# Block 2's feed-forwards in parts of 4, 6, 6 and 6 chunks, and the down weights' lower parts by an accumulating DMA

## Chip, cores and metric

One core of one Trainium2 chip. The metric is the device time in microseconds of one execution; the kernel before was run three times. The matmuls run on TensorE (PE); VectorE (DVE), ScalarE (ACT) and GpSimd (POOL) work beside it, SyncE (SP) issues loads. All names of rows are the program's.

## The reference, cut to what matters

Two transformer blocks in fp32 on 512 tokens, model width 1024. Block 1 sets 16 further tokens ahead of them (528 columns), block 2 has 512. Each block is a feed-forward, a mixer and a second feed-forward, so there are four feed-forwards (FFN1 and FFN2 in block 1, FFN3 and FFN4 in block 2), each 2816 wide:

```
D_FF = 2816
def swiglu_2(x, w_gate, w_up, w_down):
    return (jax.nn.silu(x @ w_gate) * (x @ w_up)) @ w_down
...
h = h + 0.5 * swiglu_2(rms_norm(h, ffn1_norm[l]), ffn1_w_gate[l], ffn1_w_up[l], ffn1_w_down[l])
...
h = h + 0.5 * swiglu_2(rms_norm(h, ffn2_norm[l]), ffn2_w_gate[l], ffn2_w_up[l], ffn2_w_down[l])
```

## The kernel before, in words

**Numbers in two parts.** Every fp32 operand is held as an upper part (hi, rounded to fp32r) and a lower part (lo, the rest), and each product is three matmuls: hi by hi, hi by lo, lo by hi (`mm`, L482; rows of L488). For a weight, ACT copies the raw block into hi (L120). The lower part is made in one of two ways. In the feed-forwards DVE subtracts hi from raw (L125). In the mixers, where `lo_engine` is `None`, ACT writes the negated copy of the raw (rounded like hi) into lo (L122), and a DMA that POOL issues adds the raw to it (L123, `accum_op=add`).

**The queue of weights.** `Weights` holds a list of raws in the order of use. Two raw buffers (raw_85, raw_86) take them in turn, and raw r+2 is loaded when the last unit of raw r is split. A unit (one 128-column weight block) is split by `pump` (L107) as soon as a slot, a pair of hi and lo buffers, is idle; a slot becomes idle when the matmuls of its unit are done (`free`, `release`). In the stretches of this change three whole slots turn, in the rows whi_106 with wlo_107, whi_108 with wlo_109, whi_110 with wlo_111 (and the wide pair 112/113 in FFN4); two more are cut into halves for the sevens.

**A feed-forward.** The 2816 rows are 22 chunks of 128. `PARTS` (L24) cuts them into 6, 8 and 8. For each chunk the gate and up sums are formed, `evac` makes silu(gate) times up and splits it into gh and gl; after a part's chunks, `down` (L785) multiplies them by the part's rows of the down weight: 8 column blocks, each 3 matmuls per chunk into `dn`, whose sum is added to h (`add_h`, L1321; in block 1 to y, `sum_y`, L885). `add_down` (L325) lists 4 raws with 2 units each per part.

The chunks of part 0 are full products (`run_item`: 48 matmuls of 512 columns in block 2). The chunks of later parts go by sevens (`seven`, L703): 7 products of 256-column halves in place of 8, 84 matmuls of 256 (`product`, L696; rows of L700). Their right-hand sides are made once by `prepare` (L661): 8 `normed` steps, 2 splits, 2 differences, 4 `second` steps, and 4 more splits into nh and nl, called `rest`. nh and nl hold part 0's right-hand side, so `rest` must come behind part 0's last item. In `seven` the first product's sum is copied by ACT (`ht`, L736) and the product named P6 follows in the same PSUM tile.

At the end of a part by sevens, `begin` (L775) starts the first down units on all chunks but the last while the last chunk is still being finished: one and one more in block 2, one and two more in FFN1 with its two column slices. `down` then finishes them.

**The order.** `run_ffn` (L543) runs the items left over from the lead, with `prepare`'s steps spread over the last of them, then `rest`, `down(0)`, the sevens of part 1, `down(1)` and the sevens of part 2, whose down the caller runs beside the next stage. A tile scheduler then orders each engine's instructions; that order is what the engines keep.

## Time and profile before

| what | value |
| --- | --- |
| median of three runs | 2034.89 us (2034.45 to 2038.19) |
| the profiled execution | 2036.98 us, of which its span is 2035.2 us |
| mean granted TensorE clock | 0.994 of full speed |
| instructions in the profile | 34893 |
| HBM read | 230.53 MB |

In the rows, "hi" and "lo" are tiles whi and wlo, "raw" is a weight as loaded, "dn" and "acc" are PSUM sums. Rows name an engine, a line of the program, an operation and its tile: `out<-in`.

### The profile page before, as it was taken

The page shows a single profiled execution, that of the slowest core. Times are in us where ns is not written, and L with a number is a line of the kernel's source. Part 1 is how long each engine was busy: PE and PEld are TensorE (multiplying, and loading weights), DVE is VectorE, ACT ScalarE, POOL GpSimd, SP SyncE. Part 2 cuts the span into 40 slices and gives each one's busy share as a digit, 9 for nine tenths or more (in the row PEclk, how much of TensorE's full clock was granted, in tenths as well). Part 3 has the DMA queues.
Part 4 walks back from the last instruction along what each step waited for, and adds up shares of the span by engine and source line. Part 5 has one row for each costly group of instructions (what it writes and reads, how often), then busy time and mean ns, then how long its engine had stood idle before and what let it go on. Part 6 is the DMA issues. An engine that isn't in the chain of part 4 may idle for free.

```text
span 2035.2 us, 34893 instructions
## 1 busy us (share of the span) xinstructions
PE 1995.0 (98%) x13583; PEld 1833.5 (90%) x13583; DVE 1486.4 (73%) x2949; ACT 1063.4 (52%) x2030; POOL 283.2 (14%) x290
## 2 busy tenths in 40 slices
PE   8999999999999999999999999999999999999998
PEld 8999999989989989899998998987777788898998
DVE  5948578777776767668777775876889868685784
ACT  5445345357765445445443543656878743353552
POOL 0012021023420002111000211103211100120210
PEclk9999999999999999999999999999999999999999
DMA  6357575237784238566532766737545353475761
GB/s 182 93 116 166 131 149 147 84 81 174 149 147 125 73 93 166 146 139 157 151 78 78 162 149 140 156 116 159 102 98 114 76 152 99 108 162 140 147 163 44
DMA packets 413212, 260.10 MB, mean 128 GB/s; under 512 B 17483, under 2 KB 405830, under 8 KB 413046
## 3 DMA queue, kind: packets, MB, share of 16 engines
q1 hardware_dynamic: 317446, 192.94, 32.1%
q0 software_dynamic: 95040, 63.69, 22.1%
q8 instruction: 106, 1.74, 0.3%
q10 hardware_dynamic: 560, 1.24, 0.2%
q14 instruction: 60, 0.49, 0.1%
HBM read 230.53 MB, written 4.23 MB: 115 GB/s over the span
## 4 chain that ended last, share of the span: by engine, by line
PE 84%; DVE 8%; ACT 4%; DMA 2%; issue 1%; POOL 0%; ACTq 0%; POOLq 0%; DVEq 0%; SPq 0%
PE dn L488 25%; PE sa L700 18%; PE acc L488 14%; PE sc L700 8%; PE sb L700 4%; PE accB L488 3%; PE accA L488 3%; PE wo L488 2%; DVE wlo L125 1%; ACT whi L120 1%; PE ro L1611 1%; PE p L423 1%; PE num L1202 1%; PE ms L1469 1%; DMA raw<-in_w_uq 1%
## 5 line engine op out<-in xcount | busy, mean ns | idle before, releaser
L120 ACT CAST whi<-raw 128x1024 fp32r<-128x1024 f32 (+3 forms) x500 | 397.5, 801 | 346.3 <-PE dn L488 168.5
L125 DVE TENSOR_TENSOR wlo<-raw,whi 128x512 fp32r<-128x512 f32 (+2 forms) x456 | 406.2, 905 | 134.7 <-ACT whi L120 130.6
L488 PE MATMUL dn<-gh,whi 128*128 128x256 f32 (+2 forms) x908 | 277.5, 326 | 0.6 <-ACT gh L469 0.6
L488 PE MATMUL dn<-gl,whi 128*128 128x256 f32 (+2 forms) x908 | 277.9, 326 | 0.0
L488 PE MATMUL dn<-gh,wlo 128*128 128x256 f32 (+2 forms) x908 | 277.0, 325 | 0.0
L488 PE MATMUL acc<-nh,whi 128*128 128x512 f32 (+2 forms) x600 | 191.0, 353 | 1.1 <-DVE y L1219 1.1
L488 PE MATMUL acc<-nl,whi 128*128 128x512 f32 (+2 forms) x600 | 188.5, 349 | 0.0
L488 PE MATMUL acc<-nh,wlo 128*128 128x512 f32 (+2 forms) x600 | 188.1, 348 | 0.0
L488 PEld LDWEIGHTS dn<-gh,whi 128*128 128x128 f32 x908 | 163.0, 188 | 16.5 <-ACT gh L469 0.8
L488 PEld LDWEIGHTS dn<-gl,whi 128*128 128x128 f32 x908 | 163.1, 188 | 15.5 <-DVE gl L470 0.3
L488 PEld LDWEIGHTS dn<-gh,wlo 128*128 128x128 f32 x908 | 163.2, 188 | 14.8
L700 PE MATMUL sc<-nh,whi 128*128 128x256 f32 (+1 forms) x488 | 137.4, 282 | 0.0
L700 PE MATMUL sa<-nh,whi 128*128 128x256 f32 (+1 forms) x488 | 137.3, 281 | 0.0
L700 PE MATMUL sa<-nh,wlo 128*128 128x256 f32 (+1 forms) x488 | 137.2, 281 | 0.0
L700 PE MATMUL sc<-nh,wlo 128*128 128x256 f32 (+1 forms) x488 | 137.2, 281 | 0.0
L700 PE MATMUL sc<-nl,whi 128*128 128x256 f32 (+1 forms) x488 | 137.1, 281 | 0.0
L700 PE MATMUL sa<-nl,whi 128*128 128x256 f32 (+1 forms) x488 | 137.0, 281 | 0.0
L488 PEld LDWEIGHTS acc<-nh,whi 128*128 128x128 f32 (+1 forms) x600 | 104.6, 188 | 16.4 <-DVE y L1219 1.6
L488 PEld LDWEIGHTS acc<-nh,wlo 128*128 128x128 f32 (+1 forms) x600 | 104.0, 188 | 15.0
L488 PEld LDWEIGHTS acc<-nl,whi 128*128 128x128 f32 (+1 forms) x600 | 103.9, 188 | 13.6
L95 POOL DMA_DIRECT2D raw<-in_ffn_w_up x32 | 41.1, 1284 | 448.8 <-DMA raw<-in_ffn_w_up 229.1
L95 POOL DMA_DIRECT2D raw<-in_ffn_w_in x32 | 41.1, 1283 | 439.4 <-DMA raw<-in_ffn_w_in 163.6
(494 smaller groups left out, 5583.1 us busy)
## 6 DMA issues: line engine op xcount, KB each, us to landing
raw<-in_ffn_w_in SPq DMA_DIRECT2D x56, 512.0 KB, 4.1
raw<-in_ffn_w_gate SPq DMA_DIRECT2D x44, 512.0 KB, 3.6
raw<-in_ffn_w_in SPq DMA_DIRECT2D x64, 256.0 KB, 3.2
raw<-in_ffn_w_out SPq DMA_DIRECT2D x16, 1024.0 KB, 8.0
wlo<-raw POOLq DMA_DIRECT2D x32, 512.0 KB, 5.3
raw<-in_ffn_w_up SPq DMA_DIRECT2D x64, 256.0 KB, 3.2
raw<-in_ffn_w_down SPq DMA_DIRECT2D x16, 1024.0 KB, 7.4
raw<-in_a_w_in SPq DMA_DIRECT2D x18, 512.0 KB, 3.6
```

What stands on the lines that cost most here:

```text
L95: self.nc.gpsimd.dma_start(out=dst(t), in_=src, accum_op=ALU.add)
L120: nc.scalar.copy(out=ho, in_=src)
L125: self.lo_engine.tensor_tensor(out=lw, in0=src, in1=ho.bitcast(F32), op=ALU.subtract)
L423: pe.matmul(self.p1[:, self.n:self.n + 2], lhsT=src[:, o:o + P], rhs=ones[:, 0:2], start=True, stop=True)
L488: pe.matmul(p, lhsT=w[:, k], rhs=cut(x, k, sl), start=(k == 0 and j == 0), stop=(k == last and j == 2))
L700: pe.matmul(acc, lhsT=w[:, 4 * i + k], rhs=x[:, k], start=start and k == 0 and j == 0, stop=k == 3 and j == 2, skip_group_check=not start)
L1202: pe.matmul(num[:, c0:SEQ], lhsT=w[0:kk, j], rhs=x[s_], start=(j == 0 and i == 0), stop=(j == 4 and i == 2))
L1469: pe.matmul(s, lhsT=mq[i][a][:, t0:t0 + P], rhs=mk[i][b], start=j == 0, stop=j == 2)
L1611: pe.matmul(o[i], lhsT=vt_[:, i, j], rhs=s_[i, j][b], start=(j == 0 and b == 0), stop=(j == 3 and b == 1))
```

## The change

It has two parts. First, FFN3 and FFN4 take `PARTS4`, 4, 6, 6 and 6 chunks, so that 18 of their 22 chunks go by sevens in place of 16, with four downs in place of three. With four items in part 0, three or two are used up in the lead; `run_ffn` then has one or two left, calls `prepare` before any of them, spreads the 8 `normed` steps over them, and hands the 12 other steps to `down(0)`, which runs two behind each of the first six column blocks. Second, `add_down` gets `by_dma`: in all four feed-forwards the down units of every part but the last have their lower part made as in the mixers.

```
+PARTS4 = [(0, 4), (4, 6), (10, 6), (16, 6)]
...
-    def add(self, loads, subs, halves=(), more=()):
+    def add(self, loads, subs, halves=(), more=(), by_dma=False):
...
-                if self.lo_engine is None:
+                if self.lo_engine is None or self.raws[r][3]:
                     nc.scalar.activation(out=lw, in_=src, func=ACTF.Copy, scale=-1.0)
                     nc.gpsimd.dma_start(out=lw.bitcast(F32), in_=src, accum_op=ALU.add)
                 else:
                     self.lo_engine.tensor_tensor(out=lw, in0=src, in1=ho.bitcast(F32), op=ALU.subtract)
...
-            add_down(d_ap, f0, nf)
+            add_down(d_ap, f0, nf, f0 < parts[-1][0])
...
-        run_item(items[0], slices)
+        if len(items) > 2:
+            run_item(items.pop(0), slices)
...
+        under = len(steps) if ffn.parts is PARTS else KD
...
+            down(0, (), steps[did:] + rest)
...
-        for part in (1, 2):
-            first = ffn.seven(range(PARTS[part][1]), slices if part == 1 else last)
-            if part == 1:
-                down(1, first)
+        n = len(ffn.parts) - 1
+        for part in range(1, n + 1):
+            first = ffn.seven(range(ffn.parts[part][1]), slices if part < n else last)
+            if part < n:
+                down(part, first)
...
                 for p, sl in zip(pp, slices):
                     sink(c, sl, p)
+                for f in steps[:each]:
+                    f()
+                del steps[:each]
                 W.free(1)
```

Whole program, instructions in the engines' lists: PE 13050 to 13146, DVE 2728 to 2706, ACT 1837 to 1974, POOL 281 to 369, SP 404 to 420. Of POOL's 88 more, 80 are the DMAs of L123 (8 units for each part that has them) and 8 those of the four further chunks by sevens.

**First place: ACT and POOL in the down of FFN3's second part.** Before, ACT's list where the down's units are split (the one 128x512 row belongs to the sevens that follow):

```order
L120 CAST whi_108<-raw_86 128x1024
L120 CAST whi_110<-raw_85 128x1024
L120 CAST whi_106<-raw_85 128x1024
L120 CAST whi_108<-raw_86 128x1024
L120 CAST whi_116<-raw_85 128x512
L120 CAST whi_110<-raw_86 128x1024
```

With the change:

```order
L122 CAST whi_108<-raw_86 128x768
L124 ACTIVATE wlo_109<-raw_86 128x768
L122 CAST whi_110<-raw_85 128x768
L124 ACTIVATE wlo_111<-raw_85 128x768
L122 CAST whi_106<-raw_85 128x768
L124 ACTIVATE wlo_107<-raw_85 128x768
L122 CAST whi_108<-raw_86 128x768
L124 ACTIVATE wlo_109<-raw_86 128x768
L122 CAST whi_110<-raw_86 128x768
L124 ACTIVATE wlo_111<-raw_86 128x768
```

Each copy into hi is followed by the negated copy of the same raw, and a unit now has 6 blocks of 128 columns where it had 8. POOL's list with the change, from the last loads of the sevens to the end of this down:

```order
L97 DMA raw_86<-in_ffn_w_up 128x4x128
L97 DMA rawx_12017<-in_ffn_w_gate 128x4x128
L125 DMA wlo_107<-raw_86 128x6x128
L125 DMA wlo_109<-raw_86 128x6x128
L125 DMA wlo_111<-raw_85 128x6x128
L125 DMA wlo_107<-raw_85 128x6x128
L125 DMA wlo_109<-raw_86 128x6x128
L125 DMA wlo_111<-raw_86 128x6x128
```

Before, POOL's list held only the accumulating loads of the sevens at this place:

```order
L95 DMA rawx_11984<-in_ffn_w_gate 128x4x128
L95 DMA rawx_11983<-in_ffn_w_gate 128x4x128
L95 DMA rawx_11984<-in_ffn_w_gate 128x4x128
L95 DMA raw_85<-in_ffn_w_up 128x4x128
L95 DMA raw_86<-in_ffn_w_up 128x4x128
```

So six DMAs of L125 stand in a row where POOL had nothing to issue, and two more just ahead of the piece.

**Second place: PE in the down of FFN1's second part,** from its fourth unit on (slot 110/111; the three units before were begun ahead of the last chunk). Before:

```order
L488 MATMUL dn<-gl,whi_110 128x272
L488 MATMUL dn<-gl,whi_110 128x256
L488 MATMUL dn<-gh,whi_106 128x272
L488 MATMUL dn<-gh,whi_106 128x256
L488 MATMUL dn<-gl,whi_106 128x272
L488 MATMUL dn<-gl,whi_106 128x256
L488 MATMUL dn<-gh,wlo_111 128x272
L488 MATMUL dn<-gh,wlo_111 128x256
```

With the change:

```order
L490 MATMUL dn<-gh,whi_106 128x272
L490 MATMUL dn<-gh,whi_106 128x256
L490 MATMUL dn<-gl,whi_106 128x272
L490 MATMUL dn<-gl,whi_106 128x256
L490 MATMUL dn<-gh,whi_108 128x272
L490 MATMUL dn<-gh,whi_108 128x256
L490 MATMUL dn<-gl,whi_108 128x272
L490 MATMUL dn<-gl,whi_108 128x256
L490 MATMUL dn<-gh,wlo_111 128x272
L490 MATMUL dn<-gh,wlo_111 128x256
```

Before, 8 matmuls (4 of the fourth unit, 4 of the fifth) stand ahead of the first that reads wlo_111; now 12 do (4 of the sixth too).

**Third place: DVE in FFN3's first down.** Before, the lower parts of the down's units and the sums into h:

```order
L1323 TENSOR_TENSOR h<-dn,h 128x512
L125 TENSOR_TENSOR wlo_107<-raw_85,whi_106 128x768
L1323 TENSOR_TENSOR h<-dn,h 128x512
L125 TENSOR_TENSOR wlo_109<-raw_86,whi_108 128x768
L1323 TENSOR_TENSOR h<-dn,h 128x512
```

With the change, the steps of `prepare` (ht, y, wlowide, nl) stand there:

```order
L1336 TENSOR_TENSOR h<-dn,h 128x512
L472 TENSOR_TENSOR wlowide<-ht,whiwide 128x256
L692 SCALAR_TENSOR_TENSOR ht<-y 128x256 x2
L694 SCALAR_TENSOR_TENSOR y<-ht,y 128x256
L472 TENSOR_TENSOR wlowide<-ht,whiwide 128x256
L694 SCALAR_TENSOR_TENSOR y<-ht,y 128x256
L1336 TENSOR_TENSOR h<-dn,h 128x512
L472 TENSOR_TENSOR wlowide<-ht,whiwide 128x256
L472 TENSOR_TENSOR nl<-y,nh 128x4x256 x2
L1336 TENSOR_TENSOR h<-dn,h 128x512
L472 TENSOR_TENSOR nl<-y,nh 128x4x256 x2
L127 TENSOR_TENSOR wlo_109<-raw_85,whi_108 128x1024
```

The last row is the first lower part of the sevens that follow; it stands behind the last of the splits into nl.

## Rows read from the trace of the kernel before

**Rows 1.** The page: busy time of each engine, and the chain that ended last.

```profile
PE 1995.0 (98%) x13583; PEld 1833.5 (90%) x13583; DVE 1486.4 (73%) x2949; ACT 1063.4 (52%) x2030; POOL 283.2 (14%) x290
...
PE 84%; DVE 8%; ACT 4%; DMA 2%; issue 1%; POOL 0%; ACTq 0%; POOLq 0%; DVEq 0%; SPq 0%
```

**Rows 2.** Busy times by stretch: us, PE, PEld, DVE, ACT, POOL, PEclk, DMA share, GB/s.

```profile
1054.00:1088.00 34.00, 34.00 (x151) 27.64 (x150) 32.36 (x68) 16.32 (x30) 2.57 (x2) 1.00 0.36 85
1088.00:1121.00 33.00, 33.00 (x144) 26.74 (x143) 19.97 (x30) 9.61 (x15) 0.54 (x1) 1.00 0.31 94
1121.00:1200.00 79.00, 78.59 (x651) 77.13 (x650) 63.90 (x121) 45.98 (x96) 17.59 (x14) 1.00 0.76 157
1207.50:1247.00 39.50, 39.50 (x173) 32.04 (x172) 18.41 (x25) 9.94 (x13) 3.85 (x3) 1.00 0.51 130
...
1598.60:1604.30 5.70, 4.64 (x24) 3.29 (x22) 5.27 (x11) 5.58 (x13) 2.77 (x3) 1.00 0.74 92
```

**Rows 3.** Timeline of PE, FFN3: first matmul of a stage (start us, us, row).

```profile
1054.23 0.48 PE L488 MATMUL acc<-nh,whi 128*128 128x512 f32 x1
1087.68 0.39 PE L488 MATMUL dn<-gh,whi 128*128 128x512 f32 x1
1121.08 0.28 PE L700 MATMUL sa<-xh,whi 128*128 128x256 f32 x1
1247.16 0.28 PE L700 MATMUL sa<-xh,whi 128*128 128x256 f32 x1
```

**Rows 4.** Timeline, FFN3's second part: its down's fourth unit on ACT, DVE, PE.

```profile
1213.04 2.00 ACT L120 CAST whi<-raw 128x1024 fp32r<-128x1024 f32 x2 [3.03 <-PE dn L488]
1214.58 2.35 DVE L125 TENSOR_TENSOR wlo<-raw,whi 128x1024 fp32r<-128x1024 f32 x2
1219.36 0.39 PE L488 MATMUL dn<-gh,whi 128*128 128x512 f32 x1
```

**Rows 5.** Timeline of ACT and POOL in block 2's mixer; issue to landing there.

```profile
1570.24 1.07 ACT L122 ACTIVATE wlo<-raw 128x1024 fp32r<-128x1024 f32 x1
...
1571.60 1.57 POOL L123 DMA_DIRECT2D wlo<-raw  x1 [7.75 <-ACT wlo L122]
...
DMA to landing us min/median/max: 5.7/5.8/5.9
```

**Rows 6.** DMA issues by tile, KB each, median us to landing, here and there.

```profile
raw<-in_ffn_w_gate SPq DMA_DIRECT2D x44, 512.0 KB, 3.6
...
raw<-in_ffn_w_down SPq DMA_DIRECT2D x16, 1024.0 KB, 7.4
...
wlowide<-raw POOLq DMA_DIRECT2D x1, 512.0 KB, 11.6
```

**Rows 7.** Instructions by line and form, 1054 to 1121 us: busy, mean ns, idle before.

```profile
L125 DVE TENSOR_TENSOR wlo<-raw,whi 128x768 fp32r<-128x768 f32 x8 | 7.6, 950 | 0.4 <-ACT whi L120 0.4
...
L651 DVE TENSOR_TENSOR a<-acc,r_bc 128x256 f32<-128x256 f32 x6 | 2.3, 415 | 0.0
...
L120 ACT CAST whi<-raw 128x768 fp32r<-128x768 f32 x8 | 6.7, 836 | 15.4 <-PE dn L488 10.5 <-PE acc L488 4.9
```

**Rows 8.** Timeline, FFN1's second part: its down's fourth unit and first unit.

```profile
229.10 2.95 ACT L120 CAST whi<-raw 128x1024 fp32r<-128x1024 f32 x3 [8.41 <-PE dn L488]
...
230.59 0.40 PE L488 MATMUL dn<-gh,whi 128*128 128x272 f32 x2
230.83 0.41 PE L488 MATMUL dn<-gl,whi 128*128 128x272 f32 x2
...
203.74 0.37 ACT L736 COPY ht<-sa 128x264 f32<-128x264 f32 x1
210.60 0.41 PE L488 MATMUL dn<-gh,wlo 128*128 128x272 f32 x2
```

**Rows 9.** Timeline, FFN2's second part: ACT's `ht` and the down's first unit.

```profile
831.40 0.37 ACT L736 COPY ht<-sa 128x256 f32<-128x256 f32 x1
...
837.91 0.39 PE L488 MATMUL dn<-gh,wlo 128*128 128x512 f32 x1
```

**Rows 10.** Timeline of PE: the last chunk's P6 product in FFN3, FFN4.

```profile
1194.18 0.39 PE L700 MATMUL sa<-whiwide,whi 128*128 128x256 f32 x1 [0.16 <-ACT ht L736]
1840.91 0.39 PE L700 MATMUL sa<-whi,whi 128*128 128x256 f32 x1 [0.52 <-ACT ht L736]
```

More of the change, by code (lines that the diff above doesn't have):

```diff
@@ L556, in run_ffn @@
             w_half, n_half = [(w4, 1)], 2
[L557 removed]
+        if len(items) > 2:
+            run_item(items.pop(0), slices)
         slots += [W.reserved.pop(0) for _ in range(3 - len(slots))]
         steps, rest = ffn.prepare(halves, gcol, xn, slots)
[L560 to L562 removed]
+        under = len(steps) if ffn.parts is PARTS else KD
+        did = 0
+        for i, it in enumerate(items):
+            upto = under * (i + 1) // len(items)
             run_item(it, slices, steps=steps[did:upto])
@@ L632, in two_blocks, with __init__ @@
     class Ffn:
-        def __init__(self, name, half, wide=256):
+        def __init__(self, name, half, wide=256, parts=PARTS):
+            self.parts = parts
             self.cm, self.p = open_pool(name)
@@ L639, in items @@
         def items(self, part):
-            return [Item(2, lambda sl, a, f=f: self.evac(f, sl, a[0], a[1])) for f in range(PARTS[part][1])]
+            return [Item(2, lambda sl, a, f=f: self.evac(f, sl, a[0], a[1])) for f in range(self.parts[part][1])]
         def evac(self, f, sl, g, u):
@@ L783, in finish, with down @@
             mm(list(zip(pp, slices)), u, [nf - 1], (self.gh, self.gl), last=nf - 1)
-        def down(self, nf, slices, sink, first=()):
-            first = list(first)
+        def down(self, nf, slices, sink, first=(), steps=()):
+            first, steps = list(first), list(steps)
+            each = -(-len(steps) // KD)
             for c in range(KD):
@@ L976, in two_blocks @@
         dve.tensor_scalar(out=g, in0=g, scalar1=0.5, scalar2=None, op0=ALU.mult)
-    first = run_ffn(ffn, items[3:], AB, lambda part, first: ffn.down(PARTS[part][1], AB, sum_y(part == 0), first),
+    first = run_ffn(ffn, items[3:], AB, lambda part, first, steps=(): ffn.down(ffn.parts[part][1], AB, sum_y(part == 0), first, steps),
                     [(0, TT // 2), (TT // 2, TT // 2)], V_GN[0], y, None, [A_SL])
@@ L1280, in two_blocks @@
         add_cols(d["w_o_2"][0], [(c * 256, P), (c * 256 + P, P)])
-    add_ffn(d["ffn2_w_gate_2"][0], 0, d["ffn2_w_up_2"][0], 0, d["ffn2_w_down_2"][0])
-    first = run_ffn(ffn, items[3:], [XF], lambda part, first: ffn.down(PARTS[part][1], [XF], sum_y(part == 0), first),
+    add_ffn(d["ffn2_w_gate_2"][0], 0, d["ffn2_w_up_2"][0], 0, d["ffn2_w_down_2"][0], PARTS4)
+    first = run_ffn(ffn, items[3:], [XF], lambda part, first, steps=(): ffn.down(ffn.parts[part][1], [XF], sum_y(part == 0), first, steps),
                     [XA, XB], V_GN[4], y, None, [XA])
@@ L1326, in add_h @@
         return sink
-    first = run_ffn(ffn, items[3:], [XF], lambda part, first: ffn.down(PARTS[part][1], [XF], add_h(), first), [XA, XB],
+    first = run_ffn(ffn, items[3:], [XF], lambda part, first, steps=(): ffn.down(ffn.parts[part][1], [XF], add_h(), first, steps), [XA, XB],
                     V_F1, y, None, [XF], True)
@@ L1339, in two_blocks @@
     pre = Rms(XF)
-    ffn.down(PARTS[2][1], [XF], add_h(lambda c: pre_chunk(c, XF, V_MIX, pre)), first)
+    ffn.down(ffn.parts[-1][1], [XF], add_h(lambda c: pre_chunk(c, XF, V_MIX, pre)), first)
     ffn.close()
@@ L1732, in two_blocks @@
     sq.update(pool=op_, bufs=2)
-    first = run_ffn(ffn, items[2:], ONE, lambda part, first: ffn.down(PARTS[part][1], ONE, add_h(), first), [XA, XB], V_F2,
+    first = run_ffn(ffn, items[2:], ONE, lambda part, first, steps=(): ffn.down(ffn.parts[part][1], ONE, add_h(), first, steps), [XA, XB], V_F2,
                     ob.rearrange("p a b -> p (a b)").rearrange("p (k t) -> p k t", k=KD), (wx, op_), [XA])
@@ L1763, in two_blocks @@
     us, wait = [], []
-    ks = list(range(PARTS[2][1]))
+    ks = list(range(ffn.parts[-1][1]))
     for sl in halves:
```

32 lines of the change are left out of this document (15 added, 17 removed).

## The prediction

> **What bounds the kernel.** I read the page's busy times and its chain first, then the stretches of FFN3 one by one, then the hand-overs between engines at the places that the change touches. The page says that PE is busy 98% of the span and holds 84% of the chain that ended last [rows 1]. In the stretches that the change rebuilds nothing is left over: FFN3's last items are 34.00 busy of 34.00 us, its first down 33.00 of 33.00, the sevens 78.59 of 79.00, the second down 39.50 of 39.50, at a granted clock of 1.00 [rows 2]. So fewer matmul columns is the only way to gain there, and any wait of PE is a loss in full. DVE (32.36 of 34, 63.90 of 79) and the DMA engines (0.76 of the sevens' stretch) have less room than ACT.
>
> **What the sevens save.** Three items take (1087.68 − 1054.23) / 3 = 11.15 us each, and the first down's 144 matmuls (1121.08 − 1087.68) / 144 = 0.232 us each [rows 3]. The second part, 8 sevens and 192 down matmuls, takes 1247.16 − 1121.08 = 126.08 us; less 192 × 0.232 = 44.5 that is 81.6, or 10.19 a seven. A chunk by sevens saves 0.96 us, and four chunks change over: **−3.8**. The downs have the same matmuls however the chunks are cut, with one exception: FFN4's last down works on 256 columns, at 81.6 / 672 = 0.121 us a matmul, so two chunks' 48 matmuls of 512 there cost 48 × (0.243 − 0.232) = 0.5 less: **−0.5**. The gain is thus 4.3 us, hardly more than 0.2% of the time, 4.1 us, which is about what a measurement of this kernel can tell from no change.
>
> **What a lower part costs by DMA.** DVE's subtraction was off PE's path: 1.2 us right behind ACT's copy. By DMA the chain is ACT's copy, 1.05 us for 8 blocks and 0.84 for 6 [rows 4, 7, 8]; the negated copy, 1.07; 0.29 until POOL issues; and 5.7 to 5.9 until it has landed [rows 5]. From the slot's release that is 1.05 + 1.07 + 0.29 + 5.8 = 8.2 us. For 6 blocks I need a landing that no row has. The DMA of 8 blocks keeps the 16 engines 0.74 × 5.7 = 4.2 us busy [rows 2], so 1.5 of 5.7 does not grow with size, and three quarters of 4.2 on top give 4.7: in all 0.84 + 0.84 + 0.29 + 4.7 = 6.7. Bounds for the landing: 3.6, as the plain 512 KB load has [rows 6], and 11.6, as the accumulating DMA has in a crowded stretch [rows 6]. I take the mixer's row since it is the same operation in the same form.
>
> Where does that meet PE? Three whole slots turn, so in the middle of a down each unit has two units of matmuls (11.1 us with 8 chunks, 8.4 with 6) to get ready: enough. It is tight for the fourth unit, which goes into the slot of the first. In FFN3 the copy starts at 1213.04 and PE needs the unit at 1219.36 [rows 4], and lo at the third matmul, 0.46 later: 6.8 us. By DMA at 8 blocks PE waits 8.2 − 6.8 = 1.4 us; this is FFN2's second part, which has the same form. With 6 chunks the window shrinks by a quarter of its matmuls to 21 × 0.232 + 0.46 = 5.3, against 6.7: 1.4 again, in the two middle parts of FFN3 and of FFN4. In FFN1 it is worse: three units were begun ahead, their finishes come together, and the copy of the fourth starts at 229.10 where PE wants it at 230.59 [rows 8]. The reordered list gives PE 12 matmuls ahead of lo, six pairs of 0.245 [rows 8], to 232.06; lo lands at 229.10 + 8.2 = 237.3: 5.3. Sum 1.4 + 4 × 1.4 + 5.3 = **+12.3**.
>
> The Trainium skill, "DMA: Bandwidth & Descriptors", section "Anatomy of one DMA — SWDGE (gpsimd) path", fits a DMA issued by GpSimd as 2.0 us plus bytes over 436 GB/s. By it the 512 KB would land in 3.2 us and the 6 blocks (393 KB) in 2.9, all fourth units but FFN1's would be in time, and the sum below would be about 5 in place of 16. The trace disagrees: 5.7 to 5.9 us for the same bytes [rows 5]; I go by the rows.
>
> The first unit of a part is begun right after the last chunk's P5. With 8 chunks the negated copy stands behind ACT's `ht`. FFN1: 203.74 + 0.37 + 1.06 + 0.29 + 5.8 = 211.3 against 210.60 where PE reads lo [rows 8], 0.7 late. FFN2: 831.40 + 0.37 + 1.06 + 0.29 + 5.8 = 838.9 against 837.91 [rows 9], 1.0 late. Sum **+1.7**. With 6 chunks the raw is 768 KB in place of 1024, whose load takes 7.4 us [rows 6]; it comes earlier by more than that: 0. In part 0, of 4 or 6 chunks, the units wait for their use far longer: 0.
>
> **DMA engines.** Eight lower parts of 8 blocks take 8 × 4.2 = 34 us of all engines, on top of 0.51 × 39.5 = 20 in that down [rows 2]. That is more than fits, so loads move back under the sevens, where 0.76 is used and PE still ran 78.59 of 79.00. Between nothing and 3 us for each of the six middle parts I take 0.5, near nothing by that row: **+3.0**.
>
> **ACT and POOL.** 80 more copies of 0.6 to 1.07 us, about 70 us, lie on ACT, which is busy 52% [rows 1] and 9.94 of 39.5 in the second down [rows 2]: 0 beyond the chains above. SP's 16 further loads follow from one more down per feed-forward and carry the same bytes: 0. POOL's 88 more issues, 1.57 us each [rows 5], lie on an engine 14% busy; in the downs it had 3.85 of 39.5: 0.
>
> **DVE in the short part 0.** DVE was busy 32.36 + 19.97 = 52.3 us while three items and a down of 6 ran [rows 2]. It loses the lower parts of the down, 7.6, and the evacuation of two chunks, 20 operations of 0.42 [rows 7], 8.4: 36.3 us are left for one item and a down of 4, 11.15 + 96 × 0.232 = 33.4 us. DVE is 2.9 us over, and the splits into nl stand ahead of the first lower part of the sevens. Between 0 (the excess runs on under the sevens, where DVE has 15 of 79 free) and 2.9 I take 1.5 for each of FFN3 and FFN4: **+3.0**. Each further boundary also has the last chunk's wait for `ht`, 0.16 and 0.52 [rows 10]: **+0.7**.
>
> **Sum.** −3.8 − 0.5 + 12.3 + 1.7 + 3.0 + 3.0 + 0.7 = +16.4, on the profiled 2036.98 gives 2053.4. That execution lies 2.1 above the median of 2034.89; against the median the time is **2051**.
>
> **Rivals.**
> - *The DMA lands short, and nothing waits but FFN1* (not slower). If the accumulating DMA lands like a plain load, 3.6 us [rows 6], the 8-block chain takes 6.0 of 6.8 and the 6-block one 5.6 of 5.3 or less, so these waits are at most 0.3; FFN1's fourth unit waits 3.1, the first units nothing. It decides at a landing of 3.3 us for 6 blocks and 4.4 for 8. With no cost on DVE and the DMA engines: −4.3 + 3.1 + 0.7 = −0.5, or 2034; 2031 if FFN1's wait is hidden too. For it: PE has no gap at all today, and the down stretch is only half full of DMA. Against it: 5.7 to 5.9. By the Trainium skill's page named above the landing would be shorter still.
> - *The queue is full.* In one crowded stretch the same DMA took 11.6 [rows 6]. Where the lower parts (34 of 39.5 us) meet the loads, landings grow by 5.8, and all six fourth units wait that much longer: +35, or 2086. The raw buffers would come free later too. For it: the sum of 54 in 39.5. Against: most loads can wait.
> - *DVE becomes the bound at part 0's end.* If all twelve steps end behind `down(0)` instead of beside it, PE waits for the full 2.9 and for the four splits into nl behind it, about 5 us for each feed-forward in place of 1.5: 2058. For: the twelve steps are one chain on few buffers. Against: steps of this kind ran beside items without a gap.
> - That the change doesn't do what it says is excluded by the instruction lists: two more sevens and 80 DMAs of L125 are there.
>
> **Chances.** Late lower halves 0.58, short landing 0.24, full queue 0.10, DVE 0.08. The first lies at 2043 to 2062; by its bounds a share of 0.06 ends below 2039. Of the second, 0.10 ends below 2030.8, 0.12 within 0.2%, 0.02 above. The last two are slower. So: faster 0.10, same 0.18, slower 0.72. The range 2032 to 2066 leaves out about 0.08 below, where FFN1 hides its wait too, and 0.10 above, the full queue.
>
> **What would show it.** In the changed kernel PE should have gaps of 1 to 2 us in `dn<-gh,wlo`, ended by the DMA of wlo, at the fourth unit of the middle parts, and one of some 5 us in FFN1; landings of wlo from 4.5 to 6 us; 18 sevens a feed-forward of 10.2 us; DVE some 70 us less busy and ACT some 70 more; POOL 88 DMAs more. Landings under 4 us, or no gap behind wlo, would make the forecast wrong on the fast side; landings over 8, on the slow side; gaps ended by DVE at the start of the second parts would point to the third rival.

## The result, and the profile after

| | before | after |
| --- | --- | --- |
| median | 2036.39 us (2034.45 to 2038.19, 4 runs) | 2096.46 us (2092.75 to 2106.12, 4 runs) |
| ratio | | 1.0302 [1.0282, 1.0322] |
| the profiled execution: span, mean granted clock | 2035.2, 0.994 | 2104.3, 0.986 |

The change made the kernel 3% slower, 60 us, where 16 were forecast and the range ended at 2066. The profiled execution of after is the longest of its four, 9.7 us above the median, so its sums below are some 10 us too large against the medians. Medians here and below are of fast runs; one of i4's four was a slow one of 6844 us and is left out.

The page of after: busy time of each engine, then the group of matmuls by lo, then the issues of the accumulating DMA:

```profile
PE 2017.1 (96%) x13679; PEld 1849.8 (88%) x13679; DVE 1440.5 (68%) x2921; ACT 1133.9 (54%) x2154; POOL 409.1 (19%) x378
...
L490 PE MATMUL dn<-gh,wlo 128*128 128x256 f32 (+2 forms) x898 | 283.4, 337 | 34.4 <-DMA wlo<-raw 34.3
...
wlo<-raw POOLq DMA_DIRECT2D x48, 512.0 KB, 5.7
...
wlo<-raw POOLq DMA_DIRECT2D x43, 384.0 KB, 5.4
```

Against [rows 1] PE is busy 2017.1 − 1995.0 = 22.1 us more, though it has 4.3 us less to compute, and idle 87.2 − 40.2 = 47.0 us more; the two make the 69.1 us between the spans. 34.3 us of the idle time stand ahead of matmuls by lo and were ended by the DMA that writes lo.

The landings of the page's last two lines mix places: 32 of the 48 of 512 KB are the mixers', and 16 of the 43 of 384 KB belong to first parts. In the middle downs alone the landing takes 7.2 us at the median for 512 KB and 6.5 for 384 KB, where 5.8 and 4.7 were forecast. By down, least, median and most, for FFN1's second (203 to 260 us), FFN2's second (848 to 902) and FFN3's second (1179.5 to 1215):

```profile
DMA to landing us min/median/max: 5.6/7.3/12.3
...
DMA to landing us min/median/max: 5.7/6.9/11.9
...
DMA to landing us min/median/max: 4.8/6.5/7.5
```

Where it is: the second downs of FFN1 and FFN2, a piece of the first of them, and FFN3's second down, by stretch (columns as in [rows 2]):

```profile
217.16:274.88 57.72, 47.49 (x344) 46.23 (x343) 13.10 (x27) 16.81 (x22) 12.81 (x9) 0.91 0.83 156
227.00:250.00 23.00, 18.54 (x110) 17.91 (x111) 2.22 (x6) 5.79 (x6) 4.64 (x3) 0.78 0.67 103
861.48:913.57 52.09, 43.84 (x173) 34.10 (x172) 12.31 (x20) 16.78 (x21) 11.93 (x8) 0.93 0.87 166
1193.88:1227.28 33.40, 30.43 (x132) 24.07 (x131) 12.17 (x20) 12.36 (x18) 7.58 (x6) 1.00 0.93 179
```

The same downs in the kernel before:

```profile
218.15:260.00 41.85, 41.85 (x345) 41.72 (x343) 18.76 (x32) 9.86 (x14) 3.85 (x3) 1.00 0.50 124
845.15:884.79 39.64, 39.64 (x173) 32.15 (x172) 18.57 (x26) 10.35 (x14) 3.85 (x3) 1.00 0.50 128
```

FFN1's down is 15.9 us longer and FFN2's 12.5; PE, which had no gap there, waits 10.2 and 8.2 us in them, and the same matmuls take 5.6 and 4.2 us more, at a granted clock of 0.91 and 0.93 (0.78 in the piece behind the first long waits; the two levels are 1.2 and 2.4 GHz, so some 44% of it was at the lower). The DMA engines are busy 0.83 to 0.93 of these three downs, against 0.50 in block 1's two before.

Some of PE's waits, in order: FFN1's third and fourth unit, FFN2's third, the `ht` of the last chunk ahead of FFN3's second down, and that down's fourth and seventh unit (timeline; start us, us, row, [idle before, what ended it]):

```profile
227.14 0.40 PE L490 MATMUL dn<-gh,wlo 128*128 128x272 f32 x1 [2.63 <-DMA wlo<-raw]
...
242.05 0.60 PE L490 MATMUL dn<-gh,wlo 128*128 128x272 f32 x1 [2.33 <-DMA wlo<-raw]
...
871.88 0.50 PE L490 MATMUL dn<-gh,wlo 128*128 128x512 f32 x1 [1.79 <-DMA wlo<-raw]
...
1180.50 0.58 PE L709 MATMUL sa<-whiwide,whi 128*128 128x256 f32 x1 [2.64 <-ACT ht L745]
...
1204.74 0.50 PE L490 MATMUL dn<-gh,wlo 128*128 128x512 f32 x1 [1.20 <-DMA wlo<-raw]
...
1219.28 0.50 PE L490 MATMUL dn<-gh,wlo 128*128 128x512 f32 x1 [1.76 <-DMA wlo<-raw]
```

Most of PE's new waits in the feed-forwards fall into four kinds. Fourth units of middle downs, as forecast: 2.33 in FFN1, none in FFN2, 1.20 and 1.18 in FFN3, 0.37 and 1.18 in FFN4, in all 6.3 us. Other units of the same downs: 26.3 us, of which the seventh and eighth units, made from the last raw, have 16.4 and the second and third 7.8. `ht` at the last chunk of a part, and at the first chunk behind FFN2's down: 2.64, 2.31, 0.76, 2.48, 2.84, in all 11.0. The seventh unit in the first parts' downs of FFN2, FFN3 and FFN4, and the `ht` behind the last of them: 0.57, 2.48, 2.24, 2.14, in all 7.4. The forecast's waits are there, and they are an eighth of the 51 us.

How a wait comes about that the forecast had not: the critical chain of after in FFN2's second down (start us, us, what).

```profile
864.39 7.44 DMA wlo<-raw
...
871.88 6.71 PE dn L490 x21
...
879.62 1.06 ACT wlo L124
...
881.06 5.66 DMA wlo<-raw
...
886.85 2.94 DMA raw<-in_ffn_w_in
...
901.06 5.68 DMA wlo<-raw
...
906.80 3.00 DMA raw<-in_ffn_w_in
...
910.44 7.93 DMA raw<-in_ffn_w_in
...
918.99 0.37 ACT ht L745
...
919.41 1.94 PE sa L709 x12
```

Each load of a raw begins 0.06 to 0.14 us after a lower part has landed (881.06 + 5.66 = 886.72, then the load at 886.85; 906.74, then 906.80). The accumulating DMA reads its raw until it lands, and only two raws turn; DVE's subtraction had let go of the raw 1.2 us behind ACT's copy. So the ring itself now runs at the DMA's pace. SP's issues of the down's second to fourth raw, all three and then the second alone, before:

```profile
835.59 18.23 SPq L99 DMA_DIRECT2D raw<-in_ffn_w_out  x3
...
836.73 0.37 SPq L99 DMA_DIRECT2D raw<-in_ffn_w_out  x1
```

and after:

```profile
851.19 26.78 SPq L101 DMA_DIRECT2D raw<-in_ffn_w_out  x3
...
863.64 0.37 SPq L101 DMA_DIRECT2D raw<-in_ffn_w_out  x1
```

The second of them, the raw of the fifth and sixth units, came 1.14 us behind the first and comes 12.45 behind it now, 0.12 us after the second unit's lower part landed (issued at 851.61, landed at 863.52). From the first of the three issues to the end of the third it was 18.23 us and is 26.78. The first is some 10 us ahead of the down both times (845.15, now 861.48), but the third came at 853.45, 8.3 us into the down, and comes now 16 us into it, after the landing of the fourth unit. The last landings from the down's last two raws then hold back loads of the next sevens; ACT's list has the copy of such a raw ahead of `ht`, so PE waits 2.84 us for `ht` at 919.41, and the sevens behind FFN2's down take 88.21 us in place of 83.64.

The second and third units are late for another reason: at the start of the down the transfers meet. The second unit's own landing takes 11.91 us in FFN2 and 12.35 in FFN1. The third unit's raw, the first of the three issues, can be copied 10.8 us after its issue in FFN2 (861.98) and 11.7 in FFN1, where it was 7.0 and 6.9 before.

### The profile page after: what moved, and what is told of

Read it like the earlier page. It is cut to its first block, busy times and chain, and to the rows that moved or that the text cites. A ratio compares the mean times of both kernels' runs of the same rounds, so it can differ in the third digit from the quotient of the medians.

```text
span 2104.3 us, 35472 instructions
## 1 busy us (share of the span) xinstructions
PE 2017.1 (96%) x13679; PEld 1849.8 (88%) x13679; DVE 1440.5 (68%) x2921; ACT 1133.9 (54%) x2154; POOL 409.1 (19%) x378
## 3 DMA queue, kind: packets, MB, share of 16 engines
q0 software_dynamic: 161984, 97.25, 34.3%
q8 instruction: 107, 1.75, 0.3%
## 4 chain that ended last, share of the span: by engine, by line
PE 68%; DMA 11%; DVE 7%; issue 6%; ACT 6%; POOL 1%; POOLq 0%; ACTq 0%; SPq 0%; DVEq 0%
PE sa L709 17%; PE dn L490 15%; PE acc L490 11%; PE sc L709 7%; DMA wlo<-raw 6%; PE sb L709 4%; PE accB L490 3%; DMA raw<-in_ffn_w_down 3%; PE accA L490 3%; PE wo L490 2%; ACT whi L122 1%; DMA raw<-in_ffn_w_out 1%; DVE wlo L127 1%; ACT wlo L124 1%; PE p L425 1%
## 5 line engine op out<-in xcount | busy, mean ns | idle before, releaser
L122 ACT CAST whi<-raw 128x512 fp32r<-128x512 f32 (+3 forms) x525 | 404.3, 777 | 389.6 <-PE dn L490 120.6
L127 DVE TENSOR_TENSOR wlo<-raw,whi 128x512 fp32r<-128x512 f32 (+3 forms) x408 | 344.5, 859 | 183.9 <-ACT whi L122 179.7
L490 PE MATMUL dn<-gh,wlo 128*128 128x256 f32 (+2 forms) x898 | 283.4, 337 | 34.4 <-DMA wlo<-raw 34.3
L125 POOL DMA_DIRECT2D wlo<-raw x117 | 156.0, 1403 | 548.0 <-ACT wlo L124 384.7
L490 PE MATMUL acc<-nh,whi 128*128 128x512 f32 (+3 forms) x544 | 169.5, 349 | 1.1 <-DVE y L1232 1.1
L490 PE MATMUL acc<-nl,whi 128*128 128x512 f32 (+3 forms) x544 | 166.5, 344 | 0.0
L490 PE MATMUL acc<-nh,wlo 128*128 128x512 f32 (+3 forms) x544 | 166.3, 344 | 0.0
L709 PE MATMUL sc<-nh,whi 128*128 128x256 f32 (+1 forms) x520 | 147.8, 284 | 0.0
L709 PE MATMUL sc<-nh,wlo 128*128 128x256 f32 (+1 forms) x520 | 147.5, 284 | 0.0
L490 PEld LDWEIGHTS acc<-nh,wlo 128*128 128x128 f32 (+1 forms) x544 | 93.5, 188 | 12.7
L490 PEld LDWEIGHTS acc<-nl,whi 128*128 128x128 f32 (+1 forms) x544 | 93.5, 188 | 11.1
```

Source lines behind the costliest of these rows:

```text
L122: nc.scalar.copy(out=ho, in_=src)
L125: nc.gpsimd.dma_start(out=lw.bitcast(F32), in_=src, accum_op=ALU.add)
L127: self.lo_engine.tensor_tensor(out=lw, in0=src, in1=ho.bitcast(F32), op=ALU.subtract)
L490: pe.matmul(p, lhsT=w[:, k], rhs=cut(x, k, sl), start=(k == 0 and j == 0), stop=(k == last and j == 2))
L709: pe.matmul(acc, lhsT=w[:, 4 * i + k], rhs=x[:, k], start=start and k == 0 and j == 0, stop=k == 3 and j == 2, skip_group_check=not start)
```

## The experiments

Four accounts were to be told apart. **Late**: a unit's own lower half is late (the forecast). **Held**: the raw is held until the landing, so later loads are late. **Crowded**: the DMA engines are full, so landings and loads stretch. **Parts**: the new cut of the feed-forwards costs by itself. Ratios are against runs of the kernel before that each run has of its own, on its chip. In the expectations theory 1 is Late, theory 2 is Crowded (in f5's together with Held) and theory 3 is Parts.

**1. The two parts of the change, each alone.**

```
e1_parts_alone:  add_down(d_ap, f0, nf, False)
e2_dma_alone:    PARTS4 = PARTS
e3_dma_part0:    add_down(d_ap, f0, nf, f0 == 0)
e4_dma_block2:   add_down(d_ap, f0, nf, f0 < parts[-1][0] and parts is PARTS4)
```

> 4, 6, 6 and 6 chunks in block 2, all lower parts by DVE as before. If the DMAs cost the time (theory 1: the lower part's chain is too long for the slots; theory 2: the DMA engines are full in the downs), this version keeps the 4.3 us saved and pays at most 0.7 for two more ends of a part and 3 on DVE in the short part 0: 2031 to 2037, and the waits of 2.3 to 2.8 us for ACT's ht at the ends of the 6-chunk parts are gone, since the loads have the DMA engines to themselves. If the parts themselves cost it (theory 3: less work under which to hide the loads), the five ht waits stay: about 14 us more, 2048 to 2055.

> 6, 8 and 8 chunks everywhere, the down weights of all parts but the last by DMA. Theories 1 and 2: each down in the middle pays for itself, as FFN1's (41.9 to 57.7 us) and FFN2's (39.6 to 52.1, and 4.6 in the sevens behind it) do in the changed kernel; FFN3 and FFN4 then pay about as FFN2 does, some 17 each: 2036 + 16 + 18 + 2 x 17 = 2104, from 2090 to 2110. Theory 3: block 2 pays for its parts and not for its DMAs: 2036 + 34 = 2070.

> The changed kernel with the lower parts by DMA only in the first part of each feed-forward, DVE in all others. Theories 1 and 2: the middle downs' cost is gone, and what is left are the waits in the first downs, 2.5 us in FFN3 and 2.2 in FFN4 with 1.5 to 2 at a lower clock behind each, 0.6 in FFN2: 2037 to 2046. Theory 3: the ht waits stay: 2050 to 2058.

> The changed kernel with DVE in block 1 (FFN1 and FFN2), the DMAs in block 2 alone. All theories: block 1's 34 us come back, if a down's cost stays where it is made: 2062, from 2055 to 2068. If block 1's delays were partly hidden later, less comes back: above 2070.

| run | median us | ratio |
| --- | --- | --- |
| e1_parts_alone | 2043.79 | 1.0045 [1.0032, 1.0058] |
| e2_dma_alone | 2101.97 | 1.0329 [1.0309, 1.0349] |
| e3_dma_part0 | 2052.60 | 1.0088 [1.0075, 1.0102] |
| e4_dma_block2 | 2069.80 | 1.0180 [1.0164, 1.0197] |

e2 and e3 fell into a forecast range, e1 and e4 between two. By medians, over the kernel before's 2034.49 in these runs: the parts cost 9.3 us, the first parts' DMAs 2052.6 − 2043.8 = 8.8 more, and the middle parts' DMAs 2096.5 − 2052.6 = 43.9 more; of the DMAs' cost block 1 has 2096.5 − 2069.8 = 26.7. The last two are known to some 2 us, since after was measured beside a kernel before of 2036.39. The parts were to save 4.3 us less some 3.7 of DVE and `ht`; they lose.

What they lose by shows at the last chunk of each part. PE, ACT and SP in e1 at the end of FFN3's first sevens:

```profile
1139.51 0.39 PE L709 MATMUL sa<-whiwide,whi 128*128 128x256 f32 x1 [1.33 <-ACT ht L745]
```

```profile
1137.83 1.35 ACT L122 CAST whi<-raw 128x768 fp32r<-128x768 f32 x2 [2.36 <-DMA raw<-in_ffn_w_down]
...
1139.09 0.36 ACT L745 COPY ht<-sa 128x256 f32<-128x256 f32 x1
```

```profile
1126.55 0.37 SPq L95 DMA_DIRECT2D raw<-in_ffn_w_up  x1
1127.15 0.37 SPq L95 DMA_DIRECT2D rawx<-in_ffn_w_up  x1
1131.07 0.37 SPq L101 DMA_DIRECT2D raw<-in_ffn_w_down  x1
```

ACT waits 2.36 us for a raw of the down, with `ht` behind it in its list. A raw of 6 chunks fills 1536 of the buffer's 2048 columns; the last 512 are free, and that is where the sevens load a quarter of their own raw. So the next sevens' loads are let in ahead of the down's raw. The four last chunks of the middle parts wait 1.33, 1.45, 1.75 and 1.25 us, where [rows 10] show 0.16 and 0.52.

**2. The raw put at the buffer's end**, so that nothing fits ahead of it; in f1 for all parts, in h1 for all but the first. Neither has a DMA for a lower part.

```
f1_parts_shifted:         return grid(t[:, 2048 - nf * 256:2048], nf)
h1_parts_middle_shifted:  return grid(t[:, 2048 - nf * 256:2048] if f0 else t[:, 0:nf * 256], nf)
```

> The version with the parts alone (all lower parts by DVE), but a 6-chunk down raw lies in the last 1536 columns of its buffer, not the first, so that the accumulated quarter of the next part's first sevens can no longer be loaded ahead of it. If the ht waits at the ends of the 6-chunk parts come from those early loads (they stand ahead of the down's own load on SP and share the DMA engines with it), the four waits of 1.2 to 1.7 us fall to the 0.2 to 0.5 of the kernel before: 2044 less about 5, 2039, from 2037 to 2041. If they come from the shorter parts as such, nothing moves: 2042 to 2046.

> The parts alone, all lower parts by DVE; the down raws of all parts but the first lie at the end of their buffer, those of the first part at its front as before. The last shift took away the four ht waits (5.8 us in the parts alone, 0.7 after it) and added 5 to 6 us at the start of the first sevens, whose early loads it also blocked. With the first part left at the front both should be had: 2044 less 5, 2039, from 2036 to 2041. If the early loads are needed in the middle too: 2043 or more.

f1: 2045.62, 1.0044 [1.0031, 1.0057]. h1: 2033.06 (11 runs), 0.9988 [0.9976, 1.0000]. In both the four waits at the ends are gone (0.17 us left). In f1 the first sevens of FFN3 and FFN4 begin late instead, by gaps of 3.2 and 2.9 us, since part 0's raw now keeps out loads that were useful there. SP and ACT in h1, at the place of e1's rows:

```profile
1128.30 0.37 SPq L95 DMA_DIRECT2D rawx<-in_ffn_w_up  x1
1132.19 0.37 SPq L101 DMA_DIRECT2D raw<-in_ffn_w_down  x1
```

```profile
1137.22 1.36 ACT L122 CAST whi<-raw 128x768 fp32r<-128x768 f32 x2 [0.61 <-DMA raw<-in_ffn_w_down]
```

One load fewer stands ahead, ACT can copy the down's raw 5.0 us after its issue where it was 6.8, and waits 0.61 in place of 2.36. So the parts' loss was in those early loads: 10.7 us from e1 to h1 by the medians, 12.8 when each is set against its own runs of the kernel before. h1 is the best version found, faster than both kernels by its median, though its interval reaches no change. Both expectations missed in part: f1 took the waits away and still gained nothing, since its first sevens lost as much, and h1 came out 3 us under the least that it was given.

**3. Middle DMAs taken away at one place.** The raws of a down are c = 0 to 3, two units each.

```
f5_unit3_dve:       by_dma=by_dma and (f0 == 0 or c != 1)
i1_last_raw_dve:    by_dma=by_dma and (f0 == 0 or c != 3)
i2_first_raw_dma:   by_dma=by_dma and (f0 == 0 or c == 0)
```

> The changed kernel with the second of the four raws of each middle down (its third and fourth unit) split by DVE. Theory 1 (the fourth unit's lower part is late, everything else has time): the waits on wlo at the fourth unit go, with the slower clock behind them, and little else is left but the first downs and ht: below 2070. Theory 2 (crowded DMA engines, raws held until the DMA has read them): a quarter of the DMAs is gone, so something like a quarter to a third of the middle downs' 45 us comes back, and waits on wlo stay at other units: 2080 to 2088.

> The changed kernel with the last of the four raws of each middle down (seventh and eighth unit) split by DVE. Theory of the held raws (a raw buffer is loaded again only when the DMA has read it, so the next sevens' loads start late, and with them everything that stands behind their first copy on ACT): the last raw is the one that hurts most, 2066 to 2078. Crowding alone: a quarter of the middle DMAs is gone, as in the version without the second raw's, 2079 to 2087.

> The DMA in the middle downs for the first raw only (first and second unit, split long before their use), DVE for the other three. The middle downs cost 44 us in all (2096 against 2052.6 with the first parts' DMAs alone). If each raw has its own share: 2064. If only what is late or held near the end of a down costs: 2052 to 2058.

f5: 2081.07, 1.0212 [1.0192, 1.0231], 15.4 us under after. i1: 2073.74, 1.0184 [1.0163, 1.0205], 22.7 under it. i2: 2058.70, 1.0120 [1.0078, 1.0161], 6.1 over e3, which has none of them, and whose interval overlaps. The raw that holds the third and fourth units, on the second of which the forecast rested, is worth a third of the 44 us. The last raw is worth half of them: its own two units wait 16.4 us in after, and in i1 the sevens behind FFN2's down are back at 83.53 us from 88.21 and that down at 42.7 from 52.1. One raw alone costs about 6, not far from noise, and four cost 44: the cost builds up along the ring. (i2 was expected at 2064 for equal shares, at 2052 to 2058 for a cost near the down's end.)

**4. Where the accumulating DMA reads, and how long it takes.** In g1 and i4 it reads the weight from HBM, so that no raw is held; the edit also names both ends fp32r, so source and type aren't told apart. In g4, i3 and h3 it adds one 128-column block, the unit's last, where it had four, six or eight; the other blocks keep the negated copy, so their part of the sum is left out. In h3 it does so twice, the second DMA behind the first onto the same block. i4, i3, h3 and h2 (which is after with nothing else) have h1's shift.

```
g1_from_hbm, i4_from_hbm_shifted:  nc.gpsimd.dma_start(out=lw, in_=<the unit's columns of ap>, accum_op=ALU.add)
g4_one_block, i3_one_block_shifted:
    far = slice(src.shape[1] - 1, src.shape[1])
    nc.gpsimd.dma_start(out=lw[:, far].bitcast(F32), in_=src[:, far], accum_op=ALU.add)
h3_two_blocks_in_turn:             the same line, issued twice
```

> The changed kernel, but the accumulating DMA reads the weight a second time from HBM, not from the raw buffer, so that a raw is free when ACT has read it. The bytes and the chain from slot to lower part stay. If the held raws are what stretches the downs (loads start late, and the next sevens after them): most of the loss goes, 2050 to 2070. If the crowded DMA engines or the late lower halves are: it stays, 2090 to 2105, as the same packets are moved and as late.

> The changed kernel with the accumulating DMA of a down unit cut to one block of 128 columns in place of 4, 6 or 8; the lower parts of the other blocks are left out. ACT's copies, POOL's issues, the order of all lists and every wait on a landing stay; the bytes fall to a sixth or an eighth, and a landing to about 2 us. If ACT's second copy and the waits as such cost the time: above 2075. If the length of the DMA does, by crowding, by the raws held or by lateness: near the version with the parts alone, 2044 to 2052.

> The changed kernel with the same shift of the middle and last parts' down raws. The four ht waits of the changed kernel (2.6, 2.3, 0.8 and 2.5 us) should fall to 0.2 to 0.5 each: 2096 less 7 with the clock behind them, 2089, from 2083 to 2093. If the early loads crowded the downs as well: below 2080.

> As the version before it, but each down unit's DMA is replaced by two DMAs of one block of 128 columns onto the same block, the second waiting for the first: as late as the full DMA when the engines are free (2 x 2.3 us and POOL's hand-over, 5 to 6), with a quarter to a half of its packets; the other blocks' lower parts are left out. If the lateness alone is what PE waits for (theory 1): PE waits on wlo nearly as often as with the full DMA, above 2065. If the packets crowd the engines, so that lower parts and loads land late (theory 2): most is gone, 2040 to 2052.

> The version with one block of 128 columns by DMA, with the shift of the middle raws: beside the version with two such DMAs in turn (2090) it shows what doubling the wait alone costs. If lateness and the holding of raws for that time are what counts, not bytes: its four ht waits go, 2048 less 9, 2037 to 2043, and the difference of some 50 us is the second DMA's 2.3 us of waiting, 48 times. If it also stands above 2060, the second copy on ACT or POOL's order costs it.

> The version by DMA with the shift (2119), but the DMA reads the weight from HBM, so that no raw is held. If held raws make the four waits of 4.3 to 5.7 us at the start of the sevens behind a middle down: these fall under 1 us, and the time to 2095 to 2105, though the HBM form lands later (7.1 us against 5.7). If not: 2119 to 2130.

| lower parts of the middle downs | raw at the start | raw at the end (middle parts) |
| --- | --- | --- |
| DVE | e1 2043.79; e3 (first parts by DMA) 2052.60 | h1 2033.06, 0.9988 |
| one short DMA, median landing 2.8 us in g4, 2.5 in i3 | g4 2047.74, 1.0054 [1.0038, 1.0070] | i3 2061.86, 1.0135 [1.0104, 1.0166] |
| two short DMAs in turn, 2.6 us each | | h3 2090.24, 1.0262 [1.0246, 1.0278] |
| one whole DMA | after 2096.46, 1.0302 | h2 2118.96, 1.0404 [1.0390, 1.0418] |
| one whole DMA from HBM | g1 2117.67, 1.0389 [1.0362, 1.0416] | i4 2119.27, 1.0406 [1.0370, 1.0442] |

In these runs the short DMAs, and in h1 none, hold for the first parts too. Four expectations missed: h2 was to end by 2093; i3 by 2043, or, above 2060, to blame ACT's second copy or POOL's order, and g4 speaks against the copy; i4, if held raws were the cause, by 2105; and g1 came out above both of its ranges.

g4 has every copy of ACT and every issue of POOL that after has, and no down of it waits for lo. So copies and issues alone are not the cost. What is, g4 doesn't isolate: bytes and hold shrink together, and so does the lateness, since PE reads the one block only at the unit's last chunk, 15 matmuls (3.5 us) behind the place where it wants a whole lower part of six blocks, 21 behind with eight. In the right column the time climbs over h1 by 28.8 us with one short DMA, 57.2 with two in turn and 85.9 with whole ones. h3 moves 128 KB for a lower part, where a whole one moves 384 or 512.

Most of i3's 28.8 lie at one place. The page has no wait ahead of lo, yet the start of the sevens behind each middle down of block 2 waits 5.61, 4.80, 5.95 and 4.06 us. The page's group, then PE:

```profile
L491 PE MATMUL dn<-gh,wlo 128*128 128x256 f32 (+2 forms) x898 | 276.5, 328 | 0.0
```

```profile
1190.93 0.58 PE L710 MATMUL sa<-whiwide,whi 128*128 128x256 f32 x1 [5.61 <-ACT ht L746]
```

In h2 the same wait is 4.56 us at FFN3's second sevens, and ACT's row says what it hangs on:

```profile
1223.94 0.62 ACT L122 CAST whi<-raw 128x512 fp32r<-128x512 f32 x1 [5.55 <-DMA raw<-in_ffn_w_up]
```

With the raw at the end of the buffer the sevens' quarter can't be loaded until the last lower part has landed: the second chunk's load is issued 30.6 us behind the down's start, in h1 20.9. h2's waits at the ends of parts are down to between 0.4 and 1.6 us, but those at the starts are 4.3 to 5.7. In i3 the last short DMA of FFN3's second down, behind loads of the sevens, lands 6.7 us after its issue. So even one block by DMA is dear where the shift leaves the next load no room. The shift that frees h1 costs h2 22.5 us: the early quarter that harmed the parts was what kept after from worse.

In block 1 the shift changes nothing, since 8 chunks fill the buffer. There the steps can be read without it, from the lengths of the stretches in us:

| block 1 | before | i3 | h3 | h2 | after | g1 |
| --- | --- | --- | --- | --- | --- | --- |
| FFN1, second down | 41.85 | 41.84 | 49.53 | 56.86 | 57.72 | 56.31 |
| FFN2, second down | 39.64 | 39.64 | 39.64 | 49.33 | 52.09 | 48.30 |
| FFN2, the sevens behind it | 83.64 | 84.01 | 88.74 | 86.43 | 88.21 | 83.55 |
| over before | | 0.4 | 12.8 | 27.5 | 32.9 | 23.0 |

The same code for block 1 gives 30.9 in e2 and 27.5 in h2 where after has 32.9, and 27.2 in i4 where g1 has 23.0, so these steps are known to some 5 us. One short DMA costs nothing in these three rows, and in g4, which has the same block 1, 3.9 us in the sevens behind FFN1's down. Two in turn cost 12.8 us with a quarter of a whole one's bytes, and the DMA engines are busy 0.59 of FFN1's down there: full engines aren't needed for it. But it isn't the two landings' time alone either. POOL and PE in h3's FFN1:

```profile
248.51 1.30 POOL L97 DMA_DIRECT2D raw<-in_ffn_w_in  x1 [8.37 <-DMA raw<-in_ffn_w_in]
249.26 2.34 POOL L128 DMA_DIRECT2D wlo<-raw  x2
...
259.02 0.60 PE L493 MATMUL dn<-gh,wlo 128*128 128x272 f32 x1 [4.83 <-DMA wlo<-raw]
```

POOL's list has the first DMAs of the last two units behind a load of the next sevens, which waited 8.37 us. They landed some 7 us after their issue, beside the sevens' loads, and PE then waits 4.83 us for the seventh unit. In i3 that unit's DMA stands ahead of the load (241.00, the load at 244.67). So POOL's order, the loads beside it and the landings' time are mixed in the 12.8.

g1 and i4 were to free the loads, and did: the sevens behind FFN2's down are back at 83.55 us, and i4's starts no longer wait; its sevens in block 2 take 64.8, 64.1 and 65.9 us where h2's take 71.2, 72.5 and 72.5. But the DMA from HBM lands later. FFN3's second down, least, median and most, in i4 and in h2:

```profile
DMA to landing us min/median/max: 5.8/7.9/11.1
...
DMA to landing us min/median/max: 4.8/5.9/8.5
```

In g1 the median there is 7.6 us, in after 6.5. i4's middle downs in block 2 take 40 to 46 us for h2's 35 to 37. PE has gaps of 28.6 us in these four downs. Some 16 of them end with the DMA of lo. The other 12.2 are for gh, which stands in ACT's list behind the copy of a raw that came late. ACT and PE in i4:

```profile
1189.08 0.83 ACT L122 CAST whi<-raw 128x768 fp32r<-128x768 f32 x1 [9.78 <-DMA raw<-in_ffn_w_down]
...
1193.66 0.80 PE L492 MATMUL dn<-gh,whi 128*128 128x512 f32 x1 [3.60 <-ACT gh L473]
```

That load was issued at 1175.34 and copied 13.7 us later, in h2 6.5 us after its issue, and the DMA engines are busy all of that time in i4. So the freed raws' gain is taken back by two things: landings that are longer, and loads that are slow beside a weight read twice. What a landing of 5.5 us without the hold would cost, these two runs don't show.

**5. The subtraction on POOL**, with h1's shift: no DMA, no negated copy.

```
if self.raws[r][3]:
    nc.gpsimd.tensor_tensor(out=lw, in0=src, in1=ho.bitcast(F32), op=ALU.subtract)
```

> The changed parts with the shift, and the lower parts of the down units subtracted by POOL itself, no DMA and no second copy on ACT. No row shows how long POOL takes for 128x768. Under 3.5 us it fits into the 5.3 us of the fourth unit, and DVE is relieved without a packet: 2034 to 2040. Over 5 us PE waits in every middle down: above 2050.

Expected were 2034 to 2040 if POOL took under 3.5 us. h4: 2070.67, 1.0167 [1.0153, 1.0181], 37.6 over h1 and 25.8 under after. The middle downs of block 2 are clean (29.9 to 30.8 us). The loss is in the first downs, FFN1's and FFN2's taking 41.0 and 40.9 us where they took 35.1 and 33.4, and in the sevens at whose end POOL begins to subtract, which take up to 4.6 us more. POOL's rows there and in a quiet stretch, then DVE beside the first:

```profile
736.35 4.15 POOL L124 TENSOR_TENSOR wlo<-raw,whi 128x768 fp32r<-128x768 f32 x1 [5.93 <-ACT whi L122]
...
753.35 1.84 POOL L124 TENSOR_TENSOR wlo<-raw,whi 128x768 fp32r<-128x768 f32 x1 [9.07 <-ACT whi L122]
```

```profile
738.03 0.42 DVE L696 SCALAR_TENSOR_TENSOR y<-ht,y 128x256 f32<-128x256 f32 x1
...
739.04 1.75 DVE L696 SCALAR_TENSOR_TENSOR y<-ht,y 128x256 f32<-128x256 f32 x1
```

The same operation takes POOL 1.84 us alone and 4.15 beside `prepare`'s steps; nine of DVE's steps in that time take the usual 0.41 to 0.42, and the tenth 1.75. POOL for the middle parts only was not tried.

## Why the prediction was right or wrong

**Right in direction, by other causes for the most part.** Slower had 0.72, and PE's gaps in `dn<-gh,wlo` ended by the DMA of lo are the largest new wait. But the fourth units, for which the forecast was slower, wait 6.3 us where +12.3 were summed, of 51 in all, so the direction is in part luck. FFN3's wait 1.20 and 1.18, FFN4's 0.37 and 1.18, forecast 1.4 each; FFN1's 2.33, forecast 5.3 (two waits of 0.85 and 1.14 for upper parts stand just ahead of it, 4.3 together); FFN2's none, forecast 1.4. The first units' +1.7 measured 0.20 and 0.58, in all 0.8. The range ended 30 us short of the result, because of steps that were put at nothing or next to it.

**The saving, −4.3, stands.** h1 has the same 18 sevens and downs, and PE is busy 1990.7 us in it, 4.3 less than the 1995.0 of [rows 1], at nearly the same clock (0.998 and 0.994). h1 is 3.5 us under the kernel before with what is left of DVE's and `ht`'s terms in it. DVE's +3.0 is near its size: in h1 the first parts' downs with the sevens behind them take 88.91 us in FFN3 and 87.26 in FFN4, where an undisturbed down (22.26) and the later sevens (64.31) make 86.57: 2.3 and 0.7 more, but only 0.69 us of that is a gap ended by DVE. The third rival, DVE as the bound, is out: after has no gap ended by DVE at the start of a second part.

**"The raw is 768 KB in place of 1024 … it comes earlier by more than that: 0" failed.** The smaller raw frees a quarter of the buffer, which lets other loads in ahead of it. In after the 768 KB of FFN3's second part were issued at 1170.74 and ACT could copy them at 1178.09, 7.3 us later: no sooner than the 7.4 of 1024 KB [rows 6]. The wait for `ht` at each further boundary was 1.3 to 1.8 us in e1, not the 0.16 to 0.52 behind the +0.7; keeping the early loads out (h1) gave back 10.7 us by the medians.

**"In part 0 … the units wait for their use far longer: 0" failed**, by 8.8 us (e3). In e3 the first downs of FFN3 and FFN4 take 26.60 and 26.43 us, in h1 that of FFN4 22.26: 8.5 of the 8.8. Of it 2.53 and 2.30 us are one wait each for the seventh unit's lo beside the sevens' loads, where the landing took 7.0 us and the others some 3.8; the rest are slower matmuls.

**"Three whole slots turn … enough" failed.** This step weighs most. The other units of the middle downs wait 26.3 us. The argument counted from the slot's release and took the raw to be there. But the raw's own buffer is released by the landing too, so that in a ring of two every landing delays the raw after next: FFN2's third raw was issued at 863.64, 0.12 us after a landing, 12.45 behind the second where it had been 1.14. The seventh and eighth units, whose raw comes behind the fourth unit's landing, have 16.4 us of the waits; not all of that is the hold, since some of their own landings are long (10.82 us in FFN2). The second and third units have 7.8, and there landings of some 12 us and slow loads count, not the hold.

**"SP's 16 further loads … 0", and ACT's "0 beyond the chains above", failed by the same mechanism.** SP's loads wait for landings (886.72, then 886.85), ACT's copies wait for those loads, and `ht` waits behind them in ACT's list: 11.0 us.

**"Between nothing and 3 us for each of the six middle parts I take 0.5" was too low.** The 54 us of transfers in 39.5 don't fit, as the rival of the full queue said, and loads do not simply "move back under the sevens". Of the 80 landings in the feed-forwards 30 took over 6.5 us, the longest 12.35. The landing was under-sized with it: 4.7 and 5.8 us forecast, 6.5 and 7.2 measured in the middle downs. That rival's 2086 is nearest to the result, but its mechanism, landings longer by 5.8 at the fourth units, is not what happened: in the middle downs they are 1.4 to 1.8 longer than forecast at the median. What it said in passing, that raw buffers would come free later, is what the ring shows. The short-landing rival is out: it needed 3.3 us for 6 blocks and 4.4 for 8, and the shortest took 4.77 and 5.63.

**The Trainium skill's fit** ("DMA: Bandwidth & Descriptors", section "Anatomy of one DMA — SWDGE (gpsimd) path") gives an estimate of 2.9 us for 6 blocks; the trace has 4.77 at the least for these 384 KB and 6.5 at the median of the middle downs, so it did not hold for this DMA, and the forecast was right to go by the rows.

**What stays open.** Late, held and crowded all grow with the landing. h3 shows that 12.8 of the 23 to 33 us of block 1 can come with a quarter of the bytes, but mixed with POOL's order; g1 and i4 that a freed raw gives the sevens back but not the downs; i1 that the last raw weighs most. How the 44 us of after divide among the three can't be read from these runs. Some 26 us are neither wait nor work: PE's matmuls took 22.1 us more for 4.3 less of columns. 9.8 of them lie in the two second downs of block 1, at the lowered clock; the rest was not traced to its places.

## What to carry to other kernels

When a step is moved to a DMA, count two times: when its result lands, and until when it holds its source. Where few buffers turn, the second one sets the pace of every load behind it, and reaches engines that never touch the result through their in-order lists. When a tile in a shared buffer is made smaller, ask who may now use the rest: what is let in early stands ahead of it in the queue. And a resource that is half full on average in a stretch is no proof that what is added "moves back": look at what must land in that stretch.
